# A two-block diffusion-style network on one core: squares in pairs, a gate moved behind its root, and later modulation steps

## The chip, the core and the metric

The kernel runs on one core of one Trainium2 chip. It is one program with five instruction streams: TensorE (PE, with its weight loads shown apart as PEld), VectorE (DVE), ScalarE (ACT), GpSimd (POOL) and SyncE (SP), which issues nearly all of the DMAs. The metric is the time of one execution on the device in microseconds; times shown are medians over runs, and one further execution was taken with the hardware profiler.

## The reference

The reference is two blocks of two layers each over 512 tokens of 1024 features, the first with 256 tokens of context beside them. Every layer is a norm with a modulation, a mixer, a gated residual, and in the first block a convolutional feed-forward network (FFN):

```python
mod_l = (silu_c @ ada_w[l] + ada_b[l])[:, None, :]
sh1, sc1, g1, sh2, sc2, g2 = jnp.split(mod_l, 6, axis=-1)
hl = modulate(xl, norm_mix_w[l], sh1, sc1)      # rms_norm(x, w) * (1 + scale) + shift
...
yl, yc = even_mixer(...) if l % 2 == 0 else odd_mixer(...)
xl = xl + g1 * yl
xl = xl + g2 * conv_ffn(modulate(xl, norm_ffn_w[l], sh2, sc2), ...)
...
def hgrn2_readout(o, g, onorm_w):
    o = rms_norm(o.transpose(0, 2, 1, 3), onorm_w).reshape(bsz, t_len, A_WIDTH)
    return (o * jax.nn.silu(g.astype(jnp.float32))).astype(g.dtype)
...
return rms_norm_2(x, final_g)                    # end of the second block
```

All of it is float32. The modulation is a product of one vector with a 1024 x 6144 matrix (1024 x 3072 in the second block); the matrix is read from memory once.

## The kernel before

Activations lie feature-major: 128 features on the partitions, tokens along the row, context first (256 + 512 = 768 tokens). A projection is exact to float32 by three passes: weight and activation are each split into a rounded high part and a rest, and TensorE adds wH·hH, wL·hH and wH·hL. So each weight block of 128 x 1024 is loaded by SP (`raw`), rounded by ACT (`wH`, L119) and subtracted by DVE (`wL`, L120); `W` is the stream of these blocks. `W.prep` issues the load and split of the next block, `W.take` hands a block out and calls `W.ahead(n)`, which prepares blocks until n are ready beyond the ones in use. The evacuation `evac` that is called behind the last pass of a block reads the sums from PSUM.

The stages, with their place in the span before: the norm of the inputs and first projections of mixer 0 (0 to 64 us); a weave of the gated linear attention, further projections and gates (64 to 396); its out-projection (405 to 477); the first FFN (477 to 1031); mixer 1 (1056 to 1305); the second FFN (1316 to 1665); and in the second block mixer 2 (to 2010) and mixer 3 with the final norm (to 2255).

`mixer0` begins with the squares of x0t in eight chunks, alternately on ACT (L655) and DVE (L653), and sums over the partitions by matmuls with a tile of ones, 256 and 512 tokens wide. `rsqrt` (L568) makes 1/sqrt as exp(-ln/2) on ACT (L574, L575) with one step of Newton on DVE: m (`rsm`, L573), z (`rsz`, L576), z times m (L577), r (L578). The gates come last in the weave: `evac_g` applies Silu to the projected gate (L754) and multiplies it onto o (L755). `gla.readout(h)` norms o of head h by such a root, in halves of 384 tokens. [...]

The modulation of layers to come is done beside the FFNs: a step takes a chunk of `raw` and multiplies it with the vector, one variant on DVE (L399) and one on ACT (L401) with its addition on GpSimd (L402). `ada_pace(every, start, end)` says at which modelled TensorE time (`self.pe`, in us, counted from the matmuls issued) steps are issued. `make` similarly splits certain weights early (L149 on ACT, L150 on DVE) and writes them back to memory (`make_next`, `make_every`):

```python
while self.pe >= self.make_next:
    with self.W.behind():
        next(self.make_gen, None)
    self.make_next += self.make_every
```

In the FFN, `gp` is the gate after its projection (L827), L831 to L834 are its convolution and Silu, L843 multiplies by the value (`hf`). In `finish`, the last residual's chunks (L995) are squared (L621) and added (L622), and behind the root each chunk is multiplied by its weight and the root (L1624) and sent out (L1626).

The order in which each engine does its instructions is made by a list scheduler when the program is built, from the order of the code, priorities and dependences; `issue_after(x)` keeps what stands in it behind the instruction x in that order. A changed line can therefore move its neighbours too.

## Time and profile before

| | |
|---|---|
| median of 3 runs | 2260.82 us (2260.49 to 2261.41) |
| profiled execution, its own time | 2257.02 us |
| span of the profiled execution | 2255.0 us |
| TensorE busy | 2183.5 us (97%) |
| DVE, ACT, GpSimd busy | 1548.8 us (69%), 1110.5 us (49%), 439.4 us (19%) |
| mean granted clock of TensorE | 0.991 |
| data moved | 293.92 MB, 130 GB/s on average |

The profiler records one execution; the difference of 2.0 us between its time and its span lies outside the first and last recorded instruction. In the chain of what ended last, each step is followed back to what released it. In the timeline the brackets at a row's end say how long its engine was idle before the row and which instruction released it. [...]

### The profile page before, as it was taken

To read this page: it belongs to the slowest core of one execution; us is meant where nothing else is said; L and a number is where in the kernel's file an instruction comes from. 1 tells how busy PE (TensorE), PEld (TensorE's weight loads), DVE (VectorE), ACT (ScalarE), POOL (GpSimd) and SP (SyncE) were. 2 spreads that over 40 slices of the span, in tenths; PEclk is the share of its full clock that TensorE was granted. 3 is DMA by queue.
4 is the path that set the end of the run, shared out by engine and by line. 5 is a ranking of instruction groups with operands and counts; after the bars stand their busy time and mean duration, and the time that the engine had idled before them with its cause. 6 is when DMAs were issued, how large, how long until landed. Compare 5 with 4: busy or idle time off the path is not lost.

```text
span 2255.0 us, 34813 instructions
## 1 busy us (share of the span) xinstructions
PE 2183.5 (97%) x13412; PEld 1879.8 (83%) x13412; DVE 1548.8 (69%) x2917; ACT 1110.5 (49%) x2110; POOL 439.4 (19%) x391
## 2 busy tenths in 40 slices
PE   8999999899999999999999999999999999989997
PEld 5988798798888888889889888887888887778876
DVE  5778767479766545557898685454556757868996
ACT  4444444355445434434676554343435545646772
POOL 0223222003334323330100023233210000001110
PEclk9999999999999999999999999999999999999999
DMA  9222311337776767631230135545435244122111
GB/s 329 85 94 85 103 48 48 103 108 269 247 237 214 252 217 241 207 110 50 83 99 1 38 127 163 159 143 167 152 123 198 96 142 139 38 75 80 57 48 38
DMA packets 105142, 293.92 MB, mean 130 GB/s; under 512 B 9232, under 2 KB 17424, under 8 KB 104976
## 3 DMA queue, kind: packets, MB, share of 16 engines
q1 hardware_dynamic: 104976, 291.70, 39.1%
q8 instruction: 105, 1.72, 0.3%
q14 instruction: 61, 0.50, 0.1%
HBM read 256.01 MB, written 35.65 MB: 129 GB/s over the span
## 4 chain that ended last, share of the span: by engine, by line
PE 85%; DVE 10%; ACT 3%; issue 2%; DMA 1%; POOL 1%; SPq 0%; DVEq 0%; ACTq 0%; POOLq 0%
PE b L437 81%; PE b L1306 2%; DVE wL L120 1%; DVE n_t L605 1%; DVE hL L607 1%; PE b L367 1%; PE b L1194 1%; PE b L415 0%; DVE st L1872 0%; ACT ptH L489 0%; POOL kt L1865 0%; DVE ptL L490 0%; DMA wL<-edL 0%; DVE ss L1062 0%; DVE fo L1624 0%
## 5 line engine op out<-in xcount | busy, mean ns | idle before, releaser
L437 PE MATMUL b<-hH,wH 128*128 128x256 f32 (+1 forms) x1912 | 596.6, 354 | 6.8 <-DVE hf L843 2.0
L437 PE MATMUL b<-hH,wL 128*128 128x256 f32 (+1 forms) x1912 | 592.1, 352 | 3.2 <-DVE wL L120 3.2
L437 PE MATMUL b<-hL,wH 128*128 128x256 f32 (+1 forms) x1912 | 588.2, 351 | 0.9 <-DVE hL L607 0.9
L437 PEld LDWEIGHTS b<-hH,wH 128*128 128x128 f32 x1912 | 357.1, 189 | 58.9 <-issue 7.0
L402 POOL TENSOR_TENSOR gacc<-gacc,raw 128x512 f32<-128x512 f32 x182 | 290.3, 1595 | 578.0 <-ACT raw L401 364.4
L437 PEld LDWEIGHTS b<-hH,wL 128*128 128x128 f32 x1912 | 360.8, 189 | 50.5 <-DVE wL L120 3.9
L437 PEld LDWEIGHTS b<-hL,wH 128*128 128x128 f32 x1912 | 360.1, 189 | 47.3 <-DVE hL L607 1.5
L119 ACT ACTIVATE wH<-raw 128x1024 fp32r<-128x1024 f32 (+4 forms) x238 | 244.7, 1029 | 254.2 <-PE b L437 242.7
L120 DVE TENSOR_TENSOR wL<-raw,wH 128x1024 fp32r<-128x1024 f32 (+4 forms) x238 | 298.7, 1256 | 37.4 <-ACT wH L119 35.7
L437 PE MATMUL b<-hidH,wL 128*128 128x512 f32 (+1 forms) x570 | 171.1, 344 | 0.0
L437 PE MATMUL b<-hidH,wH 128*128 128x512 f32 (+1 forms) x570 | 171.0, 344 | 0.0
L437 PE MATMUL b<-hidL,wH 128*128 128x512 f32 (+1 forms) x570 | 170.5, 343 | 0.0
L401 ACT ACTIVATE raw<-raw,csil 128x512 f32<-128x512 f32 x182 | 124.1, 714 | 57.7 <-DVE gacc L399 36.5
L437 PE MATMUL b<-yH,wH 128*128 128x256 f32 (+1 forms) x416 | 130.8, 331 | 12.6 <-ACT yH L489 12.6
L437 PE MATMUL b<-yH,wL 128*128 128x256 f32 (+1 forms) x416 | 130.5, 330 | 1.5 <-DVE wL L120 1.5
L437 PE MATMUL b<-yL,wH 128*128 128x256 f32 (+1 forms) x416 | 128.6, 328 | 0.0
L437 PEld LDWEIGHTS b<-hidH,wH 128*128 128x128 f32 x570 | 106.8, 188 | 14.9 <-issue 1.4
L437 PEld LDWEIGHTS b<-hidL,wH 128*128 128x128 f32 x570 | 107.1, 188 | 14.4 <-issue 0.2
L437 PEld LDWEIGHTS b<-hidH,wL 128*128 128x128 f32 x570 | 107.2, 188 | 13.8
L489 ACT ACTIVATE ptH<-b 128x384 fp32r<-128x384 f32 (+2 forms) x160 | 77.6, 499 | 69.4 <-PE b L1306 53.6
L490 DVE TENSOR_TENSOR ptL<-b,ptH 128x384 fp32r<-128x384 f32 (+2 forms) x160 | 89.2, 567 | 18.7 <-ACT ptH L489 17.7
L437 PE MATMUL b<-wH,hH 128*128 128x256 f32 x352 | 100.3, 286 | 1.6 <-ACT z L670 1.0
(370 smaller groups left out, 3979.0 us busy)
## 6 DMA issues: line engine op xcount, KB each, us to landing
raw<-in_weights_dram SPq DMA_DIRECT2D x199, 512.0 KB, 3.8
raw<-in_ada_w_dram SPq DMA_DIRECT2D x144, 512.0 KB, 4.3
er<-in_weights_dram SPq DMA_DIRECT2D x32, 512.0 KB, 4.5
edH<-eH SPq DMA_DIRECT2D x32, 512.0 KB, 4.9
edL<-er SPq DMA_DIRECT2D x32, 512.0 KB, 5.4
wL<-edL SPq DMA_DIRECT2D x32, 512.0 KB, 3.8
wH<-edH SPq DMA_DIRECT2D x32, 512.0 KB, 4.5
raw<-in_weights_dram SPq DMA_DIRECT2D x32, 448.0 KB, 3.5
```

The source lines that it names most:

```text
L119: self.last["H"] = nc.scalar.activation(h[:, :n], src, AF.Copy).ins
L120: self.last["L"] = nc.vector.tensor_tensor(l[:, :n], src, h[:, :n].bitcast(F32), op=ALU.subtract).ins
L367: nc.tensor.matmul(acc[32 * q:32 * q + 32, :], self.csil[:, k + a, :], raw[:, a, :, q, :], start=k + a == 0, stop=k + a == KD - 1)
L401: nc.scalar.activation(raw[:, a], raw[:, a], AF.Copy, scale=c)
L402: nc.gpsimd.tensor_tensor(acc[v], acc[v], raw[:, a], op=ALU.add)
L437: self.tail = self.nc.tensor.matmul(ps, lhsT, rhs, start=start, stop=stop, **kw).ins
L489: self.nc.scalar.activation(h, src, AF.Copy)
L490: self.nc.vector.tensor_tensor(l, src, h.bitcast(F32), op=ALU.subtract)
L605: nc.vector.scalar_tensor_tensor(t, x(j, s, e), A[:, j, v:v + 1], r, op0=ALU.mult, op1=ALU.mult)
L607: nc.vector.scalar_tensor_tensor(hL[j][:, s:e], t, b, h.bitcast(F32), op0=ALU.add, op1=ALU.subtract)
L1194: nc.tensor.transpose(ps[:, c], P[:, a, c], self.ident)
L1306: self.nc.tensor.transpose(ps[:, k * 128:(k + 1) * 128], P[:, k * 128:(k + 1) * 128], self.ident)
```

## The change

Six edits. (1) The squares of the first norm are added in pairs on DVE before the sums with ones, which makes eight such matmuls in place of sixteen; ACT now does six of the squares. (2) `rsqrt` issues Ln before m, takes a list of PSUM halves with one Exp over both, and keeps its Exp in `self.root`. (3) The last gate's Silu goes into tiles of its own (`z`) and is issued behind the Exp of the last readout, whose root is done in one piece. (4) `lin` calls `W.ahead(2)` behind the first evacuation of a first group that goes over all tokens at once (the out-projections). (5) The modulation steps of the FFNs start at 26 and 18 us instead of 8 and come every 6.9 us instead of 7.2; `make` starts at 26 instead of 2 and goes every 6.5 instead of 6.9. (6) In the final norm ACT multiplies the last 256 tokens by the weight as they come, and behind the root DVE does four multiplications of 512 columns instead of eight of 256.

```diff
@@ -464,6 +464,8 @@
                     with self.tc.high_priority(100):
                         for i in blocks:
                             evac(b0 + i, ps[i], part)
+                            if parts is segs and i == 0:
+                                self.W.ahead(2)
                 if end and after:
                     after(part[0])
 
@@ -570,9 +572,12 @@
         nc = self.nc
         w = r.shape[-1]
         m, z = scratch or (pool.tile([128, w], F32, name="rs" + i, tag="rs%s%d" % (i, w), bufs=1) for i in "mz")
-        nc.vector.tensor_scalar(m, x, -4.0 / n, -4 * EPS, op0=ALU.mult, op1=ALU.add)
-        nc.scalar.activation(r, x, AF.Ln, bias=self.eps[:, 0:1], scale=1.0 / n)
-        nc.scalar.activation(r, r, AF.Exp, bias=self.eps[:, 1:2], scale=-0.5)
+        xs = x if isinstance(x, list) else [x]
+        c = w // len(xs)
+        for i, v in enumerate(xs):
+            nc.scalar.activation(r[:, i * c:(i + 1) * c], v, AF.Ln, bias=self.eps[:, 0:1], scale=1.0 / n)
+            nc.vector.tensor_scalar(m[:, i * c:(i + 1) * c], v, -4.0 / n, -4 * EPS, op0=ALU.mult, op1=ALU.add)
+        self.root = nc.scalar.activation(r, r, AF.Exp, bias=self.eps[:, 1:2], scale=-0.5).ins
         nc.vector.tensor_tensor(z, r, r, op=ALU.mult)
         nc.vector.tensor_tensor(z, z, m, op=ALU.mult)
         nc.vector.scalar_tensor_tensor(r, z, 3.0, r, op0=ALU.add, op1=ALU.mult)
@@ -648,13 +653,16 @@
                 self.ada_load(nt, 12) if n == 4 else self.W.load()
         sums = [self.aux()[:, :e - s] for s, e, _, _ in SEG2]
         for j in range(KD):
-            sq = nt.tile([128, T], F32, name="n_sq", tag="n_sq", bufs=3)
-            if j % 2:
+            sq = nt.tile([128, T], F32, name="n_sq", tag="n_sq", bufs=4)
+            if j in (1, 5):
                 nc.vector.tensor_tensor(sq, xt[:, j], xt[:, j], op=ALU.mult)
             else:
                 nc.scalar.activation(sq, xt[:, j], AF.Square)
-            for (s, e, _, _), ps in zip(SEG2, sums):
-                self.mm(ps, self.ones, sq[:, s:e], j == 0, j == KD - 1)
+            if j % 2:
+                nc.vector.tensor_tensor(sq, prev, sq, op=ALU.add)
+                for (s, e, _, _), ps in zip(SEG2, sums):
+                    self.mm(ps, self.ones, sq[:, s:e], j == 1, j == KD - 1)
+            prev = sq
         r = nt.tile([128, T], F32, name="n_r")
         for (s, e, _, _), ps in zip(SEG2, sums):
             self.rsqrt(nt, r[:, s:e], ps, D)
@@ -750,7 +758,10 @@
 
         def evac_g(b, ps, part):
             for s, e, bank, _ in SEG2:
-                t = gt.tile([128, 512], F32, name="ut", tag="ut", bufs=1)
+                if b < 3:
+                    t = gt.tile([128, 512], F32, name="ut", tag="ut", bufs=1)
+                else:
+                    t = gt.tile([128, T], F32, name="z", tag="z", bufs=4)
                 nc.scalar.activation(t[:, :e - s], ps[:, bank, :e - s], AF.Silu)
                 nc.vector.tensor_tensor(o[:, b, s:e], o[:, b, s:e], t[:, :e - s], op=ALU.mult)
 
@@ -768,7 +779,14 @@
         self.psum(("mm", "aux"), mm=(0, 2, 1, 3), aux=(4, 6, 5))
         fill = itertools.chain(project(1), mixed(0), project(2), gated("u", 0, evac_u), project(3), mixed(1),
                                *[gated("u", i, evac_u) for i in range(1, 4)], *[gated("g", i, evac_g) for i in range(3)])
-        self.run(lin_v(0), self.weave(attend(), self.mixed_in(fill, self.ada_pe(24), 6.8), 178.0), gated("g", 3, evac_g))
+        self.run(lin_v(0), self.weave(attend(), self.mixed_in(fill, self.ada_pe(24), 6.8), 178.0))
+        root = self.root
+
+        def evac_g3(b, ps, part):
+            with self.tc.issue_after(root):
+                evac_g(b, ps, part)
+
+        self.run(gated("g", 3, evac_g3))
         self.close("h0")
         self.close("gt")
         self.dump("og", o)
@@ -860,10 +878,10 @@
             return ev
 
         total = 3 * NF * KD * 3 * T / 2400
-        self.ada_pace(7.2, 8.0, total - 16.0)
+        self.ada_pace(6.9, (26.0, 18.0)[l], total - 16.0)
         self.side, self.ada_fetch = self.open("side", n.side), True
         if l == 0:
-            self.make_gen, self.make_next, self.make_every = self.W.make(self.side, self.dram), self.pe + 2.0, 6.9
+            self.make_gen, self.make_next, self.make_every = self.W.make(self.side, self.dram), self.pe + 26.0, 6.5
         i0 = 0
         for gi, G in enumerate(FFN_GROUPS):
             st["H"], st["L"] = [], []
@@ -1613,16 +1631,26 @@
 
         nc = self.nc
         nt = self.open("nt", "right")
-        add, rstd = self.sumsq(nt, TL, self.xl)
+        sumsq, rstd = self.sumsq(nt, TL, self.xl)
+        fo = [nt.tile([128, 2, 256], F32, name="fo", tag="fo", bufs=8) for _ in range(8)]
+
+        def add(j, s, e):
+            sumsq(j, s, e)
+            if e == TL:
+                nc.scalar.activation(fo[4 + j // 2][:, j % 2], self.xl(j, TL - 256, TL), AF.Copy,
+                                     scale=self.vec("final_g", j, 1))
 
         def after(part):
             s, e, _, _ = part
             r = rstd(part)
             for j in range(0, KD, 2):
-                o = nt.tile([128, 2, 256], F32, name="fo", tag="fo", bufs=4)
-                for i in range(2):
-                    nc.vector.scalar_tensor_tensor(o[:, i], self.xl(j + i, s, e), self.vec("final_g", j + i, 1), r,
-                                                   op0=ALU.mult, op1=ALU.mult)
+                o = fo[j // 2 + (4 if s else 0)]
+                if s:
+                    nc.vector.tensor_tensor(o, o, r[:, None, :].to_broadcast([128, 2, 256]), op=ALU.mult)
+                else:
+                    for i in range(2):
+                        nc.vector.scalar_tensor_tensor(o[:, i], self.xl(j + i, s, e), self.vec("final_g", j + i, 1), r,
+                                                       op0=ALU.mult, op1=ALU.mult)
                 nc.sync.dma_start(self.out[:, j:j + 2, s:e], o)
 
         return SimpleNamespace(add=add, after=after)
@@ -1921,8 +1949,11 @@
 
             def ev():
                 r = big("qe")
-                for i, ps in enumerate(box["ps"]):
-                    self.rsqrt(pool, r[:, i * 384:(i + 1) * 384], ps, 128, [half_t("e", 2) for _ in range(2)])
+                if h < 3:
+                    for i, ps in enumerate(box["ps"]):
+                        self.rsqrt(pool, r[:, i * 384:(i + 1) * 384], ps, 128, [half_t("e", 2) for _ in range(2)])
+                else:
+                    self.rsqrt(pool, r, box["ps"], 128, [big(n, 2) for n in ("kc", "qc")])
                 nc.vector.scalar_tensor_tensor(o[:, h], o[:, h], self.vec("onorm"), r, op0=MUL, op1=MUL)
 
             return [(sq, pe, ev)]
```

Line numbers of the changed program are higher, by 2 to 31, than those of the one before. Below, rows stand in each engine's program order.

ACT at the end of the weave, before: the last readout's squares `ks`, then its roots in halves (`qe`), with the gate's Silu (`ut`) and a weight split.

```order
ACT_TABLE_LOAD
L574 ACTIVATE qe<-b_4106,eps 128x384
L575 ACTIVATE qe<-qe,eps 128x384
ACT_TABLE_LOAD
L754 ACTIVATE ut<-b_4134 128x256
ACT_TABLE_LOAD
L574 ACTIVATE qe<-b_4107,eps 128x384
L119 ACTIVATE wH<-raw 128x1024
L575 ACTIVATE qe<-qe,eps 128x384
ACT_TABLE_LOAD
L754 ACTIVATE ut<-b_4136 128x512
L489 ACTIVATE yH<-ym 128x768 x4
```

The same place in the changed program; `z` is the last gate's Silu, `ym` the first input of the out-projection.

```order
L1943 ACTIVATE ks<-o 128x768
ACT_TABLE_LOAD
L578 ACTIVATE qe<-b_4102,eps 128x384
L578 ACTIVATE qe<-b_4103,eps 128x384
L580 ACTIVATE qe<-qe,eps 128x768
ACT_TABLE_LOAD
L765 ACTIVATE z<-b_4124 128x256
L765 ACTIVATE z<-b_4126 128x512
L119 ACTIVATE wH<-raw 128x1024
L491 ACTIVATE yH<-ym 128x768 x4
```

Two loads of function tables less stand there, both halves of Ln and one Exp of 768 stand ahead of the Silus, and the weight split went behind them.

DVE early in the first FFN, before: the rest of the norm's hL, then `make`'s L150, modulation (L399), the convolution of two gates and the weight split that the next matmuls need.

```order
L607 SCALAR_TENSOR_TENSOR hL<-n_t,mods,hH 128x256 x2
L150 TENSOR_TENSOR er<-er,eH 128x1024
L399 SCALAR_TENSOR_TENSOR gacc<-raw,csil,gacc 128x512
L831 TENSOR_SCALAR a<-gp_4965,vecs 128x769
L399 SCALAR_TENSOR_TENSOR gacc<-raw,csil,gacc 128x512
L832 SCALAR_TENSOR_TENSOR a<-gp_4965,vecs,a 128x769
L831 TENSOR_SCALAR a<-gp_4966,vecs 128x769
L833 SCALAR_TENSOR_TENSOR a<-gp_4965,vecs,a 128x769
L832 SCALAR_TENSOR_TENSOR a<-gp_4966,vecs,a 128x769
L150 TENSOR_TENSOR er<-er,eH 128x1024
L833 SCALAR_TENSOR_TENSOR a<-gp_4966,vecs,a 128x769
L120 TENSOR_TENSOR wL<-raw,wH 128x1024
```

The same place in the changed program, where L849 to L851 are the convolution steps that were L831 to L833.

```order
L612 SCALAR_TENSOR_TENSOR hL<-n_t,mods,hH 128x256 x2
L849 TENSOR_SCALAR a<-gp_4955,vecs 128x769
L850 SCALAR_TENSOR_TENSOR a<-gp_4955,vecs,a 128x769
L849 TENSOR_SCALAR a<-gp_4956,vecs 128x769
L851 SCALAR_TENSOR_TENSOR a<-gp_4955,vecs,a 128x769
L850 SCALAR_TENSOR_TENSOR a<-gp_4956,vecs,a 128x769
L120 TENSOR_TENSOR wL<-raw,wH 128x1024
L851 SCALAR_TENSOR_TENSOR a<-gp_4956,vecs,a 128x769
L150 TENSOR_TENSOR er<-er,eH 128x1024
```

The two L150 and two L399 that stood ahead of the weight split are behind it.

TensorE at the end of the first sums, before (`n_sq` with ones are the sums, `raw` with csil the modulation, `hH` the first projection).

```order
L437 MATMUL b_130<-n_sq,ones 128x256
L437 MATMUL b_131<-n_sq,ones 128x512
L367 MATMUL b_181<-raw,csil 32x64 x32
L367 MATMUL b_222<-raw,csil 32x64 x32
L367 MATMUL b_270<-raw,csil 32x64 x32
L367 MATMUL b_307<-raw,csil 32x64 x32
L437 MATMUL b_365<-hH,wH 128x256
```

And in the changed program, from the third pair on.

```order
L437 MATMUL b_130<-n_sq,ones 128x256
L437 MATMUL b_131<-n_sq,ones 128x512
L367 MATMUL b_177<-raw,csil 32x64 x16
L437 MATMUL b_130<-n_sq,ones 128x256
L437 MATMUL b_131<-n_sq,ones 128x512
L367 MATMUL b_177<-raw,csil 32x64 x16
L367 MATMUL b_218<-raw,csil 32x64 x32
L367 MATMUL b_266<-raw,csil 32x64 x32
L437 MATMUL b_361<-hH,wH 128x256
L437 MATMUL b_363<-hH,wH 128x512
L367 MATMUL b_303<-raw,csil 32x64 x16
L437 MATMUL b_361<-hH,wL 128x256
```

Half of the first modulation group now stands ahead of the last pair's sums, and the fourth group is spread over the first projection's passes.

## Rows read from the trace of the kernel before

**Rows 1.** The page: busy time of TensorE, and the chain by engine.

```profile
PE 2183.5 (97%) x13412; PEld 1879.8 (83%) x13412; DVE 1548.8 (69%) x2917; ACT 1110.5 (49%) x2110; POOL 439.4 (19%) x391
...
PE 85%; DVE 10%; ACT 3%; issue 2%; DMA 1%; POOL 1%; SPq 0%; DVEq 0%; ACTq 0%; POOLq 0%
```

**Rows 2.** Windows: length; busy PE, PEld, DVE, ACT, POOL; clock, DMA share, GB/s.

```profile
6.50:20.00 13.50, 13.48 (x36) 7.55 (x38) 3.38 (x5) 2.85 (x4) 0.00 (x0) 1.00 1.05 383
20.00:30.30 10.30, 5.61 (x257) 4.65 (x256) 8.95 (x20) 6.40 (x11) 0.00 (x0) 0.80 1.07 370
30.30:45.90 15.60, 15.57 (x183) 12.60 (x183) 10.48 (x16) 6.69 (x9) 0.00 (x0) 0.92 1.04 386
```

**Rows 3.** Timeline of the start: start, duration, instruction, count, idle before and releaser.

```profile
6.51 13.52 PE L437 MATMUL b<-n_sq,ones 128*128 128x256 f32 x32 [6.51 <-ACT n_sq L655]
...
30.33 1.01 PE L437 MATMUL b<-hH,wH 128*128 128x256 f32 x2 [0.28 <-ACT hH L489]
```

**Rows 4.** The tile x0t: instructions (ns min/median/max, first and last start), landing.

```profile
L640 SPq DMA_DIRECT2D x0t<-in_xT_dram x4: 420/428/652, 1.2 to 2.6; - x4
L655 ACT ACTIVATE n_sq<-x0t x4: 842/842/843, 5.6 to 14.9; 128x768 f32<-128x768 f32 x4
L653 DVE TENSOR_TENSOR n_sq<-x0t x4: 957/958/959, 5.6 to 16.3; 128x768 f32<-128x768 f32 x4
...
DMA to landing us min/median/max: 4.4/6.6/8.7
```

**Rows 5.** Timeline of the last gate.

```profile
389.62 1.45 PE L437 MATMUL b<-ks,ones 128*128 128x384 f32 x4
...
397.16 0.58 ACT L574 ACTIVATE qe<-b,eps 128x384 f32<-128x384 f32 x1 [1.31 <-issue]
...
401.64 1.02 DVE L1926 SCALAR_TENSOR_TENSOR o<-o,vecs,qe 128x768 f32<-128x768 f32 x1
...
403.15 0.60 ACT L754 ACTIVATE ut<-b 128x512 f32<-128x512 f32 x1 [3.96 <-DVE o L755]
403.78 0.69 DVE L755 TENSOR_TENSOR o<-o,ut 128x512 f32<-128x512 f32 x1 [0.66 <-ACT ut L754]
...
405.46 1.01 PE L437 MATMUL b<-yH,wH 128*128 128x256 f32 x2 [9.79 <-ACT yH L489]
```

**Rows 6.** Windows, as Rows 2, behind the gate.

```profile
405.50:408.20 2.70, 2.70 (x9) 2.31 (x10) 2.70 (x4) 2.70 (x4) 0.00 (x0) 0.50 0.60 234
```

**Rows 7.** Timelines of DVE and TensorE in the first FFN.

```profile
501.09 1.22 DVE L150 TENSOR_TENSOR er<-er,eH 128x1024 fp32r<-128x1024 f32 x1 [4.97 <-ACT eH L149]
...
512.03 1.21 DVE L120 TENSOR_TENSOR wL<-raw,wH 128x1024 fp32r<-128x1024 f32 x1
...
513.30 0.50 PE L437 MATMUL b<-hH,wL 128*128 128x512 f32 x1 [2.11 <-DVE wL L120]
```

**Rows 8.** Windows, as Rows 2, of the first FFN.

```profile
477.00:520.00 43.00, 40.88 (x286) 38.03 (x285) 36.53 (x62) 23.70 (x42) 5.08 (x5) 0.96 0.57 196
520.00:620.00 100.00, 100.00 (x609) 86.74 (x608) 80.60 (x83) 50.37 (x69) 36.43 (x23) 1.00 0.74 256
```

**Rows 9.** Timelines of DVE and TensorE in the second FFN.

```profile
1337.23 1.52 DVE L831 TENSOR_SCALAR a<-gp,vecs 128x512 f32<-128x512 f32 x1
...
1342.05 0.51 PE L437 MATMUL b<-hH,wH 128*128 128x512 f32 x1 [1.96 <-DVE hf L843]
```

**Rows 10.** Timelines of TensorE and DVE in mixer 2's out-projection.

```profile
1994.42 0.68 DVE L622 TENSOR_TENSOR n_acc<-n_acc,n_sq 128x512 f32<-128x512 f32 x1
...
1994.56 0.50 PE L437 MATMUL b<-yH,wL 128*128 128x512 f32 x1 [1.50 <-DVE wL L120]
```

**Rows 11.** Timelines of TensorE, ACT and DVE in the tail.

```profile
2244.85 0.70 PE L437 MATMUL b<-n_acc,ones 128*128 128x256 f32 x2 [1.93 <-DVE n_acc L622]
...
2246.05 0.47 ACT L574 ACTIVATE n_r<-b,eps 128x256 f32<-128x256 f32 x1 [1.86 <-DVE rsm L573]
...
2248.48 3.26 DVE L1624 SCALAR_TENSOR_TENSOR fo<-xlat,vecs,n_r 128x256 f32<-128x256 f32 x8
```

## Prediction

> **What bounds the kernel now.** I read the page first: TensorE is busy 97% of the span, and 85% of the chain that ended last is its matmuls, nearly all at L437 [rows 1]. The change removes almost no TensorE work: 8 of 16 sums with ones in the start, four of which are 512 wide. So it can only gain where TensorE waits or runs at its lower clock. The second reading is therefore the list of TensorE's waits, and the third the clock by windows. Five places matter for this change, and in each the reader is to see who ended the wait: the start, where TensorE is full but with sums that nothing else can pass [rows 2, 3]; the last gate, one wait of 9.79 us [rows 5]; the first FFN, 2.11 us [rows 7]; the second FFN and the out-projection of the third mixer, 1.96 and 1.50 us [rows 9, 10]; and the tail after the last projection [rows 11].
>
> **Start: squares in pairs (gain 4.5 us, between 1.5 and 6).** From 6.5 to 20 us TensorE is busy 13.48 of 13.50 us, with 32 records of the sums in 13.52 us, 0.42 each [rows 2, 3]. After the change there are 16. They no longer set the pace: the last of the four transfers of x0t lands 2.6 + 8.7 = 11.3 us in; behind it stand two squares on ACT (0.84 each) and one addition on DVE, which I price as DVE's square of the same size, 0.96 [rows 4]. So the last pair is ready at 11.3 + 1.7 + 1.0 = 14.0, and its four records (1.7 us at 0.42, 3.4 at twice that, since the first sums go slower) end at 15.7 to 17.4, against 6.51 + 13.52 = 20.03. I take 16.9, some 3.1 earlier. The four additions cost DVE 3.8 us, and the two more squares on ACT 1.7: both lie under the landings. Behind the sums the first projection began at 30.33, 10.3 us after them [rows 3]. There DVE now takes the norm's products ahead of the weight split (1.21, [rows 7]) and ACT's Ln no longer stands behind rsm; that is worth another 1 to 2 us, so the projection begins some 5 earlier. Is its data there? The DMA engines are full until 45.9 (share 1.04 to 1.07, 370 to 386 GB/s, [rows 2]) and the order of the transfers is the same. Up to the end of that stretch the program takes x0t (3.1 MB), 16 pieces of modulation and three of weights (0.52 MB each) and 0.2 MB of vectors: 13.3 MB, at 0.38 MB/us about 35 us, and with the first 2.5 us 38, an estimate from those rows. TensorE was there at 45.9. The floor leaves 8 us, so it doesn't bind at the end; on the way, TensorE's new order puts half of a modulation group between two matmuls of the first projection, and waits there for its transfer. I take off half a microsecond for that: 4.5.
>
> TensorE's clock was granted at 0.80 in 20 to 30.3 and 0.92 in 30.3 to 45.9 [rows 2]. [...]
>
> **Last gate behind the root (gain 6.5 us, between 4.5 and 7.5).** Before: the sums of the last readout end at 391.07. The root goes in two halves; ACT puts a Silu between them, and Ln of the second half begins only at 397.16, with 1.31 us in which it waited for nothing shown, as behind a change of function. Then o at 401.64 (1.02 us), then the second Silu, which had waited 3.96 us for the multiplication that frees the one `ut` buffer, its multiplication at 403.78 (0.69), and TensorE goes on at 405.46 [rows 5]. After: Ln, Ln, one Exp of 768 and both Silus in a row. The first Ln begins when its sums end, about 390.5 (two of the four records); two at 0.58 and an Exp of 768, which I price at 0.85 between Silu's 0.60 for 512 and o's 1.02 for 768: root at 392.7. DVE's four steps of 768 at 1.02 end at 396.8, while ACT does the Silus into buffers of their own and one weight split. The two multiplications, 0.69 and about 0.4, end at 397.9. In before, TensorE began 1.0 us after the multiplication ended (405.46 - 404.47); that gives 398.9, or 6.55 earlier. The weight split that DVE now has between the gate and yL (1.21) puts yL at 400; TensorE has two passes of the first chunk before it needs yL, at half clock 1.6 us (398.9 to 400.5), so it hides; if it doesn't, it costs up to 1. I count the half clock behind the wait (405.5 to 408.2, granted 0.50, [rows 6]: 1.35 us) as still lost; if the shorter wait spares it, the gain goes to 7.5. The sum counts one thing more as zero: two changes of ACT's function fewer, since they are inside these times.
> By the row, a change costs 1.31 of idle. [...]
>
> **Later steps in the first FFN (gain 3.6, between 0 and 4.5).** DVE idles 4.97 us at 496 to 501, because the first `make` step L150 stands ahead of L831 and its input has only just come. All of DVE's queue is then late: wL runs 512.03 to 513.24, TensorE waits 2.11 us for it [rows 7], and the clock of that stretch is 0.96 of 43 us, 1.7 lost [rows 8]. With make from 26 us and modulation from 26, DVE's rows go from hL straight to L831: that spares the 4.97 of idle time and two L150 steps (1.22 each) and two of L399 ahead of wL. The gate's input, not DVE, then sets the end; wL would come some 3 us earlier, before the matmul that waited. I count 2.11 + 1.5. The same steps are now done in less time: every 6.9 and 6.5 instead of 7.2 and 6.9, with as many of them, so DVE's load rises by some 5% later on. DVE is busy 80.6% where it is fullest (520 to 620), and TensorE 100% [rows 8]: the room is 19%, so I price the denser pace at zero, and at rival 4 if the cover is gone.
>
> **Second FFN (gain 1.0, between -1 and 2).** L831 took 1.52 us at 1337.23, while GpSimd makes the additions of a modulation step, where another DVE step of that size takes 0.68 [rows 10]; hf is then late, and TensorE waits 1.96 [rows 9]. Modulation from 18 instead of 8 takes these additions away there. Against it, DVE's new order has two weight splits (1.21 each) between the steps of the norm just ahead. Net 1.0.
>
> **W.ahead(2) (gain 1.5, between 0 and 1.8).** At 1994.56 TensorE waits 1.50 for a wL that stands behind four residual additions and is late [rows 10]. Now the splits for the next two blocks are issued after the first evacuation; the other projections of this form had no such wait. The residuals behind it come 1.2 us later, and only the norm's squares wait for them.
>
> **Tail (gain 1.4, between 1.0 and 1.8).** Ln began at 2246.05, though the sums ended at 2245.55: Ln ahead of rsm gives 0.46. Behind the root eight multiplications take 3.26 [rows 11]; four of 512 columns at 0.68 with some overlap, as DVE's addition of that size [rows 10], take 2.5: 0.8. Two fewer ahead of the last n_acc: 0.2. ACT's eight extra multiplications lie in its waits (1.86 in that row).
>
> Ln first in the other norms, and the scheduler's new orders in the weave and the mixers, I count as zero: none of these places is edited, and a single late instruction there is worth what one was elsewhere, 1.5 to 2.1 us [rows 7, 9, 10]; two of them either way make the bounds, 4 less or 4 more.
>
> **Sum:** 4.5 + 6.5 + 3.6 + 1.0 + 1.5 + 1.4 = 18.5. The profiled execution took 2257.0 us (span 2255.0 and 2.0 around it), so 2238.5; the median of the runs shown is 3.8 above that execution, which gives 2242.3: I predict 2242.
>
> **The rivals.** (1) The start's gain is given back: with half the sums TensorE idles between pairs, stays at half clock through the 5 us of projection behind them, and waits for the pieces of modulation. For it: the clock of 0.80 after idling [rows 2]. Against: the first projection was at half clock already. Gain 1.5 instead of 4.5: 2245.3; 13%. (2) At the gate TensorE then waits for yL behind the weight split, or Ln still behind a change of function: 4 instead of 6.5, 2244.8; 10%. (3) The change doesn't do what it says outside the gate: other orders of DVE bring new waits in the weave and the mixers, as many as the FFN terms save; that leaves the start, the gate and the tail less 4, 2252; 12%. (4) The other side: DVE's cover in the first FFN fails. There each late wL costs what the one at 513 did, 2.11 + 1.7 = 3.8. Five of them undo the gain of 18.5; from the seventh the kernel is slower by over 0.2% (4.5 us, about what a measurement of this kernel can tell from no change). At eight: 2273. For it: the pace is denser over all of 500 us. Against: no such wait from 520 to 620 at 80.6%. Undone 4%, slower 4%. (5) More than the sum: the half clock is spared at the gate, and the reorders help: 2238; 7%.
>
> **Numbers.** The forecast has 50%, by itself 2239 to 2246. The range takes in rivals 1, 2, 3 and 5 and leaves out rival 4 and the edges: 2236 to 2252. Faster 0.92, same 0.04, slower 0.04.
>
> **What the profile after would show.** Start: 16 records of sums, ended before 17.5, and the stretch that ended at 45.9 ending near 41. Gate: Ln, Ln, Exp without a Silu between, TensorE again by 399.3 less what the start gained. FFN: no wait at the first wL, clock near 1.00 there. Out-projection: no 1.5 us wait. Tail: four multiplications, some 10.6 us from TensorE's last projection matmul to the end instead of 12.1. The prediction is wrong if TensorE's waits of the same size stand elsewhere, above all before wL in the first FFN, or if the start ends above 43.

## The result, and the profile after

The changed kernel takes 2235.26 us (median of 4 runs, 2230.33 to 2236.51) against 2261.11 us: a ratio of 0.9881 with an interval of 0.9864 to 0.9898, 23 to 31 us less. The forecast was 2242 us, with a range of 2236 to 2252. The direction was right, the time lies just below the range, and two of the sum's terms were far off in opposite directions.

The page of the changed kernel: span, busy time of the engines, chain by engine.

```profile
span 2233.8 us, 34775 instructions
...
PE 2177.2 (97%) x13396; PEld 1875.4 (84%) x13396; DVE 1551.3 (69%) x2912; ACT 1117.5 (50%) x2119; POOL 443.5 (20%) x391
...
PE 80%; DVE 9%; issue 7%; ACT 2%; DMA 1%; POOL 0%; DVEq 0%; SPq 0%; ACTq 0%; POOLq 0%
```

TensorE's busy time fell by 6.3 us against [rows 1], the span by 21.2. So about 15 us came out of waits. Stage by stage, the start gave nothing. Windows of its first 46 us, columns as in [rows 2]:

```profile
7.80:17.00 9.20, 9.13 (x61) 4.57 (x65) 3.83 (x4) 4.67 (x7) 0.00 (x0) 1.00 1.06 378
17.00:20.00 3.00, 1.56 (x96) 1.23 (x87) 2.44 (x8) 2.49 (x4) 0.00 (x0) 1.00 1.02 388
20.00:30.30 10.30, 5.99 (x134) 4.41 (x134) 9.72 (x17) 6.37 (x9) 0.00 (x0) 0.67 1.07 370
30.30:45.90 15.60, 15.60 (x196) 11.71 (x187) 7.29 (x12) 4.09 (x6) 0.00 (x0) 1.00 1.05 391
```

TensorE's timeline there, where [rows 3] had one block of sums and the projection at 30.33:

```profile
7.82 6.86 PE L437 MATMUL b<-n_sq,ones 128*128 128x256 f32 x12 [7.82 <-DVE n_sq L662]
...
15.32 1.56 PE L437 MATMUL b<-n_sq,ones 128*128 128x256 f32 x4
...
22.04 0.65 PE L367 MATMUL b<-raw,csil 128*32 128x64 f32 x32 [3.11 <-DVE gacc L373]
24.29 1.08 PE L367 MATMUL b<-raw,csil 128*32 128x64 f32 x32 [1.60 <-DMA raw<-in_ada_w_dram]
25.45 1.01 PE L437 MATMUL b<-hH,wH 128*128 128x256 f32 x2
...
45.64 0.64 PE L367 MATMUL b<-raw,csil 128*32 128x128 f32 x16
```

The sums are 16 records, done by 16.9, and the projection begins at 25.45, 4.9 us earlier. But TensorE now waits 3.11 and 1.60 us for pieces of the modulation, which come no earlier (the fifth and sixth land at 21.9 and 24.2 us, before at 21.4 and 22.9), the clock of 20 to 30.3 is 0.67 instead of 0.80, and the modulation that the second half of the norm needs ends at 46.3, where it ended at 45.9 before.

The last gate, ACT, DVE and TensorE, against [rows 5]:

```profile
388.47 1.45 PE L437 MATMUL b<-ks,ones 128*128 128x384 f32 x4
389.31 1.23 ACT L578 ACTIVATE qe<-b,eps 128x384 f32<-128x384 f32 x2 [1.99 <-PE b L437]
...
390.57 0.94 ACT L580 ACTIVATE qe<-qe,eps 128x768 f32<-128x768 f32 x1
...
394.31 0.87 ACT L765 ACTIVATE z<-b 128x256 f32<-128x256 f32 x2 [2.80 <-PE b L437]
394.52 1.02 DVE L1957 SCALAR_TENSOR_TENSOR o<-o,vecs,qe 128x768 f32<-128x768 f32 x1
...
397.66 0.61 PE L437 MATMUL b<-yH,wH 128*128 128x256 f32 x2 [3.15 <-ACT yH L491]
```

Ln over both halves, one Exp, the Silus behind it, and a wait of 3.15 us instead of 9.79. From the first matmul of the sums with ones to the first of the out-projection it is 9.19 us instead of 15.84: 6.65 less, where the forecast had 6.55.

In the first FFN TensorE is idle for 0.1 us in all, so nothing is left of the wait of [rows 7]; in the second none of [rows 9] is. In the out-projection of mixer 2, the third of the four mixers, the wait for wL of [rows 10] is gone. TensorE's waits from 1960 to 1990 us (line, releaser, us in total, times, longest):

```profile
PE b L437 <- ACT yH L491: 2.8, 1, 2.8
PE b L437 <- ACT ptH L491: 0.2, 1, 0.2
```

The tail, TensorE, ACT and DVE against [rows 11], and then the DMA view of 2227 to 2233.8, GB/s in 40 slices, and the four last issues with their size and time to landing:

```profile
2224.04 0.70 PE L437 MATMUL b<-n_acc,ones 128*128 128x256 f32 x2 [1.77 <-DVE n_acc L627]
...
2224.78 0.47 ACT L578 ACTIVATE n_r<-b,eps 128x256 f32<-128x256 f32 x1 [0.85 <-PE b L437]
...
2227.20 2.50 DVE L1649 TENSOR_TENSOR fo<-fo,n_r 128x512 f32<-128x512 f32 x4
...
GB/s 0 0 0 0 0 0 0 0 0 0 36 307 331 301 379 350 319 307 392 344 307 331 373 343 338 337 361 343 313 54 0 0 0 0 0 0 0 0 0 0
...
out_dram<-fo SPq DMA_DIRECT2D x4, 256.0 KB, 2.5
```

Ln starts 0.04 us after the sums and four multiplications take 2.50, as priced. The last four transfers of 256 KB then run without a break at some 340 GB/s, 0.77 us each, while DVE delivers one every 0.63 (one every 0.82 before, by [rows 11]). From the first multiplication to the end it is 6.6 us now and 6.5 to 6.6 before, so the quicker multiplications gain nothing at the end, where the queue is now the slower of the two.

### The profile page after: what moved, and what is told of

It reads as the page before. It is cut to its first block, busy times and chain, and to the rows that moved or that the text cites. A ratio compares the mean times of both kernels' runs of the same rounds, so it can differ in the third digit from the quotient of the medians.

```text
span 2233.8 us, 34775 instructions
## 1 busy us (share of the span) xinstructions
PE 2177.2 (97%) x13396; PEld 1875.4 (84%) x13396; DVE 1551.3 (69%) x2912; ACT 1117.5 (50%) x2119; POOL 443.5 (20%) x391
## 4 chain that ended last, share of the span: by engine, by line
PE 80%; DVE 9%; issue 7%; ACT 2%; DMA 1%; POOL 0%; DVEq 0%; SPq 0%; ACTq 0%; POOLq 0%
PE b L437 77%; PE b L1324 1%; DVE wL L120 1%; PE b L367 1%; DVE hL L612 1%; DVE n_t L610 1%; PE b L1212 1%; PE b L415 0%; DVE st L1900 0%; DVE z L1739 0%; ACT ptH L491 0%; DVE ss L1080 0%; DVE ptL L492 0%; DVE e L1886 0%; PE b L1787 0%
## 5 line engine op out<-in xcount | busy, mean ns | idle before, releaser
L849 DVE TENSOR_SCALAR a<-gp,vecs 128x769 f32<-128x769 f32 (+1 forms) x44 | 30.0, 681 | 139.7 <-ACT gp L845 139.7
```

The source lines that it names most:

```text
L849: nc.vector.tensor_scalar(a, gp[:, 1:1 + L], cw(1, i), cb(i), op0=ALU.mult, op1=ALU.add)
```

## The experiments

Each stage runs from its first matmul to that of the next; in the kernel before, the bounds are 0, 65.2, 389.6, 405.5, 475.5, 1103.8, 1313.5, 1695.4, 1950.9 and 2016.9 us, so the first FFN's row takes in the first projections of mixer 1. All are single profiled executions. Two of the same kernel differ by up to 1.5 us in a stage (the first two columns) and by 2.0 in the start (the two runs without pairs below, 63.7 and 65.7), so only larger differences are read. The columns with Ln first have 12 of TensorE's records, some 2 us of work at the stage's mean of 0.2 each, behind the bound at 1695 instead of ahead of it (1825 or 1826 in the second FFN's stage, elsewhere 1837 or 1838); the second FFN and mixer 2 are therefore read together.

| us | before | before again | pairs | gate only | Ln only | Ln and gate | steps only | all, m first | all |
|---|---|---|---|---|---|---|---|---|---|
| start | 65.2 | 64.5 | 65.8 | 64.4 | 65.7 | 64.4 | 64.5 | 66.6 | 65.3 |
| weave | 324.4 | 323.4 | 324.1 | 326.0 | 323.3 | 323.8 | 324.1 | 325.2 | 323.1 |
| last gate | 15.8 | 15.8 | 15.8 | 9.8 | 11.5 | 9.2 | 15.8 | 9.8 | 9.2 |
| out-projection 0 | 70.0 | 70.6 | 70.3 | 70.3 | 70.7 | 71.1 | 70.0 | 70.6 | 71.1 |
| first FFN | 628.3 | 629.6 | 628.9 | 629.2 | 627.2 | 627.2 | 624.7 | 624.0 | 623.0 |
| mixer 1 | 209.7 | 210.6 | 209.6 | 209.6 | 209.4 | 208.9 | 209.8 | 209.9 | 210.3 |
| second FFN | 381.8 | 381.8 | 383.4 | 384.6 | 376.0 | 376.6 | 378.4 | 378.8 | 376.7 |
| mixer 2 | 255.6 | 254.7 | 255.5 | 254.6 | 256.0 | 255.9 | 254.8 | 254.7 | 255.3 |
| these two together | 637.4 | 636.6 | 638.9 | 639.1 | 632.0 | 632.4 | 633.2 | 633.4 | 632.0 |
| mixer 2's out-projection | 66.0 | 64.5 | 64.8 | 64.8 | 63.1 | 63.5 | 64.8 | 63.5 | 61.3 |
| mixer 3 and tail | 238.2 | 238.0 | 239.3 | 239.5 | 238.3 | 236.6 | 239.1 | 238.3 | 238.5 |
| **timed, ratio to before** | 1 | 1.0001 | 1.0000 | 0.9977 | 0.9925 | 0.9922 | 0.9971 | 0.9923 | 0.9881 |

**The kernel before, again.** No edit.

> The kernel before, unchanged, once more. Theory A (its first profiled execution, 2257.0 us, was a quick draw): ratio 1.000, and this profile is 2259 to 2261 us, longer than the first by stretches at half clock and by waits whose length changes, not by other instructions. Rival B (the profiler takes some 4 us off this kernel, but none off the changed one): again 2256 to 2258 us, at the same places.

The timed ratio is 1.0001 (0.9991 to 1.0012), the profile 2255.68 us, the lowest of ten runs between that and 2264.64. Theory A's 2259 was missed, and B is not shown either: other profiles (2259.39 with the pairs alone, 2235.58 of the changed kernel) lie a little above their medians, and another execution of this kernel, not the profiled one, took 2255.74. What follows is narrower: one profiled execution of this kernel can lie 4 us below its median. Whether the 3.8 us that the prediction carried over from before to after was a draw stays open, since both profiles of this kernel lie 4 to 5 us low; in the changed kernel it is not there.

**The start.** Pairs alone; then the changed kernel without pairs, twice, the second time beside the changed kernel on one chip; then the changed kernel with one pair's sums only.

```diff
 # pairs alone (in part; the whole is in the diff of the change)
...
+            if j % 2:
+                nc.vector.tensor_tensor(sq, prev, sq, op=ALU.add)
...
 # one pair only: the sums of the other three are left out, the divisor is D // 4
-                for (s, e, _, _), ps in zip(SEG2, sums):
-                    self.mm(ps, self.ones, sq[:, s:e], j == 1, j == KD - 1)
+                for (s, e, _, _), ps in zip(SEG2, sums) if j == KD - 1 else ():
+                    self.mm(ps, self.ones, sq[:, s:e], True, True)
...
```

> The kernel before with the pairs of squares alone. Theory A (the start's end is set by the pieces of modulation, which come when they came, and by TensorE's order behind them, so that sums done earlier only make TensorE idle earlier): the first projection begins near 25.5 us instead of 30.3, the weave near 65.3 as in both kernels, and the time is within 1 us of before. Rival B (the pairs gain what the prediction gave them, and another edit took it back): the weave begins 4 to 5 us earlier and the time is 4.5 us less.

> The changed kernel with the squares as before, one sum with ones for each chunk. Theory A (the pairs gain nothing anywhere): the weave begins within 1 us of 65.3, and the time is within 2 us of the changed kernel's, 2234 to 2237. Rival B (the pairs are worth their 4.5 us in the changed kernel, where other edits spend it): 2239 to 2241.

> The changed kernel once more, beside the same without pairs on one chip. Theory A (the pairs are neutral): both within 1 us of each other. Rival B (the pairs cost: TensorE idles 4 us more in the start and the clock falls there and in the weave): this one 1.5 to 3 us slower than the one without pairs. Its ratio to before 0.987 to 0.990.

> The changed kernel with the squares as before, a second time, now beside the changed kernel. Theory A: within 1 us of it. Rival B: 1.5 to 3 us less, and the better version of the two; the weave begins near 64 us.

> The changed kernel, where only the last pair goes through the sums with ones; the other three pairs are left out of the norm's sum, and its divisor is a quarter. Theory A (TensorE's work ahead of 30 us is not what ends the start): the weave still begins at 65 to 65.5 us, though 12 of 16 records of the sums are gone. Rival B (these sums are on the path): it begins 1 to 5 us earlier.

Pairs alone: ratio 1.0000 (0.9991 to 1.0010). Without pairs 0.9880 (0.9866 to 0.9895), and the second time 0.9883 (0.9868 to 0.9898) beside 0.9887 (0.9871 to 0.9904) for the changed kernel: 2232.80 and 2233.36 us. With one pair's sums alone a single run took 2234.24 us. The pairs neither gain nor cost. With pairs alone the projection begins at 26.56 (expected near 25.5) and the weave at 65.8, and without them the weave of the changed kernel begins at 63.7, earlier than expected, and at 65.7. With one pair's sums alone the sums still end at 17.2, since they cannot begin before the last squares, and the projection begins at 25.44 as in the changed kernel: that run takes work from TensorE, but brings nothing earlier. Windows of the start with pairs alone:

```profile
0.00:20.00 20.00, 10.57 (x144) 5.97 (x144) 9.06 (x18) 8.15 (x13) 0.20 (x4) 1.00 0.95 341
20.00:30.30 10.30, 5.47 (x113) 3.96 (x117) 9.70 (x17) 6.33 (x9) 0.00 (x0) 0.67 1.07 370
30.30:45.90 15.60, 15.60 (x200) 11.76 (x192) 7.30 (x12) 4.09 (x6) 0.00 (x0) 1.00 1.05 392
45.90:65.80 19.90, 17.83 (x164) 14.68 (x163) 10.30 (x17) 12.54 (x19) 3.27 (x4) 1.00 0.50 166
```

And with one pair's sums alone:

```profile
0.00:20.00 20.00, 5.83 (x124) 3.77 (x128) 8.56 (x17) 8.34 (x13) 0.20 (x4) 1.00 0.94 340
20.00:30.30 10.30, 7.33 (x149) 5.49 (x141) 8.90 (x18) 6.20 (x8) 0.00 (x0) 0.57 1.08 372
30.30:45.90 15.60, 15.60 (x191) 11.73 (x183) 8.16 (x13) 4.09 (x6) 0.00 (x0) 0.96 1.05 390
45.90:65.70 19.80, 17.42 (x163) 14.32 (x161) 10.22 (x17) 12.46 (x19) 4.06 (x4) 1.00 0.48 164
```

The first window shows what is taken from TensorE: 13.48 us busy before, 10.57, then 5.83. From 30.3 to 45.9 it is busy throughout in both, as in [rows 2], and the weave begins at 65.8 and 65.7 against 65.2. TensorE's idle time up to there is 12.2, 16.3 and 19.6 us: with the pairs what the sums no longer take is idled. The clock of 20 to 30.3 is 0.80, 0.67 and 0.57, but from 20 to 45.9 the pairs lose no more by it (length times one less the clock: 3.3 us before, 3.4 with pairs, 5.1 with one pair): the stretch at half clock (granted 0.50, from 26.1 to 32.9 us before, from 23.3 to 30.1 in the changed kernel) only comes earlier. In these three profiles the clock of 20 to 30.3 is the lower the less TensorE did up to 20 us (13.48, 10.57 and 5.83); why is not shown.

**The roots and the gate.** Ln ahead of m alone; that with the gate edit; the gate edit with m first; and all six edits with m first.

```diff
 # Ln only (rsqrt); "m first" has the two lines of the loop the other way round
-        nc.vector.tensor_scalar(m, x, -4.0 / n, -4 * EPS, op0=ALU.mult, op1=ALU.add)
-        nc.scalar.activation(r, x, AF.Ln, bias=self.eps[:, 0:1], scale=1.0 / n)
...
+        for i, v in enumerate(xs):
+            nc.scalar.activation(r[:, i * c:(i + 1) * c], v, AF.Ln, bias=self.eps[:, 0:1], scale=1.0 / n)
+            nc.vector.tensor_scalar(m[:, i * c:(i + 1) * c], v, -4.0 / n, -4 * EPS, op0=ALU.mult, op1=ALU.add)
...
 # gate
+                    self.rsqrt(pool, r, box["ps"], 128, [big(n, 2) for n in ("kc", "qc")])
...
+            with self.tc.issue_after(root):
+                evac_g(b, ps, part)
```

> The kernel before with Ln ahead of m in every root and the last gate behind one root of 768. Theory A (the gate's term was right): the 9.79 us wait becomes some 3.2, the out-projection's first matmul comes 6.6 us earlier plus up to 1 us from the weave, and the tail 0.5 less: 7 to 8 us less. Rival B (the orders of the weave and the later stages, which move with it, gain as much again): over 10 us less.

> The kernel before with nothing but Ln ahead of m in every root. Theory A (what the run with Ln and gate gained behind the gate comes from Ln: in the second FFN's norm DVE then does its three root steps between the weight splits instead of behind them): the waits of 0.93, 0.66 and 1.96 us in the second FFN shrink to under 1 us together, that FFN takes some 377 us instead of 382, the gate still waits 9.8, and the whole is 6 to 9 us less. Rival B (the gate moved the schedule of all that follows by chance): the second FFN stays at 382 and the whole is within 2 us of before.

> The changed kernel with m ahead of Ln again in every root, the other edits kept. Theory A (Ln ahead of m is the largest part, and shares the second FFN's waits with the later steps): the gate waits 4 to 5 us instead of 3.15, the FFNs lose 1 to 3 us, the third mixer's out-projection 1 to 2, the tail 0.5: slower than the changed kernel by 5 to 10 us, 2240 to 2246. Rival B (the order in the roots matters only where the later steps and the gate are not changed): within 2 us of the changed kernel.

> The kernel before with the last gate behind one root of 768, m still ahead of Ln. Theory A (the gate edit by itself gives what was predicted for it less the 0.5 us that Ln ahead saves): the wait of 9.79 becomes 3.5 to 4.5, the FFNs and the third mixer are as before, 5 to 7 us less. Rival B (most of the gate's gain came from Ln as well): 2 to 3 us less, with a wait over 6 us.

The pair of edits gave 0.9922 (0.9908 to 0.9937), over twice what theory A had, so Ln was run alone: 0.9925 (0.9910 to 0.9940), some 17 us, where 6 to 9 were expected. The gain comes with Ln's two lines and needs no gate edit. The gate alone gave 0.9977 (0.9966 to 0.9987), 5 us, with a wait of 3.74; and all edits but Ln 0.9923 (0.9909 to 0.9938), 2243.04 us, 8 to 10 slower than the changed kernel on that chip (its gate waits 3.74, where 4 to 5 were expected). But the two lines also change the order that the list scheduler makes around them. With Ln alone the gate had been expected to keep its wait of 9.8 us; it waits 5.42:

```profile
391.01 1.11 ACT L578 ACTIVATE qe<-qe,eps 128x384 f32<-128x384 f32 x2
...
394.89 0.38 ACT L757 ACTIVATE ut<-b 128x256 f32<-128x256 f32 x1 [2.76 <-PE b L437]
...
400.51 1.01 PE L437 MATMUL b<-yH,wH 128*128 128x256 f32 x2 [5.42 <-ACT yH L489]
```

Both Ln and both Exp now stand ahead of the first Silu, which the gate edit was to bring about. So 4.4 us at the gate come with Ln alone by a new order; where the gate edit fixes the order, Ln or m first makes 0.6 there (9.2 and 9.8). No run swaps the two reads and keeps all else in place. What the swap itself does is seen in the second FFN's norm. Before: the sums, then DVE, then ACT.

```profile
1315.83 0.70 PE L437 MATMUL b<-n_acc,ones 128*128 128x256 f32 x2
...
1317.67 1.27 DVE L607 SCALAR_TENSOR_TENSOR hL<-n_t,mods,hH 128x256 fp32r<-128x256 f32 x3
1318.86 0.42 DVE L573 TENSOR_SCALAR rsm<-b 128x256 f32<-128x256 f32 x1
1319.19 2.35 DVE L120 TENSOR_TENSOR wL<-raw,wH 128x1024 fp32r<-128x1024 f32 x2
1321.46 0.42 DVE L576 TENSOR_TENSOR rsz<-n_r 128x256 f32<-128x256 f32 x1
...
1319.31 0.47 ACT L574 ACTIVATE n_r<-b,eps 128x256 f32<-128x256 f32 x1 [1.01 <-DVE rsm L573]
```

With Ln alone:

```profile
1310.08 0.70 PE L437 MATMUL b<-n_acc,ones 128*128 128x256 f32 x2
...
1310.87 0.46 ACT L576 ACTIVATE n_r<-b,eps 128x256 f32<-128x256 f32 x1
...
1312.31 0.42 DVE L577 TENSOR_SCALAR rsm<-b 128x256 f32<-128x256 f32 x1
...
1313.04 0.41 DVE L579 TENSOR_TENSOR rsz<-n_r 128x256 f32<-128x256 f32 x1
1313.38 1.22 DVE L120 TENSOR_TENSOR wL<-raw,wH 128x1024 fp32r<-128x1024 f32 x1
1314.51 0.41 DVE L580 TENSOR_TENSOR rsz<-rsz,rsm 128x256 f32<-128x256 f32 x1
```

Before, rsm stands in DVE's row behind the norm of other chunks and starts 2.3 us after the sums; Ln waits for it (1.01), Exp for Ln, and the first step on the root stands behind two weight splits. With Ln first, ACT starts 0.09 us after the sums, and rsm follows where DVE has room. Of the stage's 5.9 us less, TensorE's waits are 3.1, and the 12 records that run behind its bound some 2. The tile view of rsm in the kernel before says how much waited for it in all (us, times):

```profile
  ACT n_r L574: 22.0, 12
```

With Ln alone nothing waits for rsm any more, and DVE waits for Ln, 6.5 us in 4 times; with all edits but Ln it is 20.0 us in 12 again. The 22 us are ScalarE's idle time and no price: the gain was 17 alone and 8 to 10 beside the other edits. The order with m first holds in the gate edit, where Ln stands behind both rsm, here in `kc`:

```profile
391.26 1.20 DVE L576 TENSOR_SCALAR kc<-b 128x384 f32<-128x384 f32 x2 [2.90 <-PE b L437]
...
391.85 1.23 ACT L577 ACTIVATE qe<-b,eps 128x384 f32<-128x384 f32 x2 [2.61 <-DVE kc L576]
...
400.19 0.76 PE L437 MATMUL b<-yH,wH 128*128 128x256 f32 x2 [3.74 <-ACT yH L489]
```

Here m and Ln read the same sums and neither reads what the other writes, but the one that stands second is seen to wait for the other (Ln for m 22.0 us in 12 times with m first, m for Ln 6.5 us in 4 with Ln first), so the one that the longer chain needs belongs first. Why it waits is not shown.

**Later steps.** Edit 5 alone.

```diff
-        self.ada_pace(7.2, 8.0, total - 16.0)
+        self.ada_pace(6.9, (26.0, 18.0)[l], total - 16.0)
...
-            self.make_gen, self.make_next, self.make_every = self.W.make(self.side, self.dram), self.pe + 2.0, 6.9
+            self.make_gen, self.make_next, self.make_every = self.W.make(self.side, self.dram), self.pe + 26.0, 6.5
```

> The kernel before with the later modulation and make steps alone. Theory A (both FFNs gain by it, and more than predicted): the first FFN 5 to 6 us, the second 4 to 5 (the waits of 1.96, 0.93 and 0.66 us go together), 10 to 11 us less. Rival B (this edit gives the predicted 4.6, and the rest of what the FFNs gained came from Ln standing ahead in their norms): 4 to 5 us less, with the waits of 0.93 and 0.66 in the second FFN's norm still there.

0.9971 (0.9958 to 0.9985): 3 to 9 us, between the theories. The first FFN takes 4 to 5 us less (its wait of 2.11 for wL is gone), the second 3 to 4. In its norm stood, before, two waits besides the one of [rows 9]:

```profile
1324.68 0.39 PE L437 MATMUL b<-hH,wH 128*128 128x256 f32 x1 [0.93 <-ACT hH L606]
...
1329.02 0.39 PE L437 MATMUL b<-hL,wH 128*128 128x256 f32 x1 [0.66 <-DVE hL L607]
```

With the later steps alone 1.96 and 0.66 are gone, and of 0.93 half is left:

```profile
1319.35 0.39 PE L437 MATMUL b<-hH,wH 128*128 128x256 f32 x1 [0.48 <-ACT hH L606]
```

The L831 of 1.52 us in [rows 9] is one of 22 of that size in the second FFN; it alone runs beside a GpSimd addition, and the others take 0.50 to 0.55. With the later steps such a long one (1.54) stands at 1341.6, where TensorE does not wait for it.

**Earlier splits.** `W.ahead(2)` alone, as in the diff of the change.

> The kernel before with the earlier splits of two blocks alone. Theory A: the wait of 1.2 to 1.5 us for wL in the third mixer's out-projection goes, and a loss at half clock with it: 1.5 to 3 us less. Rival B (the residuals and squares that come later cost as much): within 1 us.

0.9993 (0.9983 to 1.0002), a median 2.1 us lower: unclear. In its profile the wait for wL is gone, and the out-projection takes 62.4 us, 2 to 4 less than in the five runs with m first and without this edit (63.5 in the one with m first and all other edits). The tail's edit was not run alone; but from its sums on the tail takes 9.7 us with Ln alone and 9.8 with all edits, 10.2 before.

## Why the prediction was wrong

The step that failed on one side is the start. That "the projection begins some 5 earlier" was right; that the stage then ends 4.5 earlier was not. I counted the bytes up to the end of the stretch, found room and stopped there. The count held (the sixteenth piece of the modulation lands at 39.6 us, by the estimate 38); what I left out is TensorE's own work behind the earlier start. Up to the end of that piece it now has 192 records of the modulation and 63 of the projection, before 128 and 55, and runs 4.7 us of them at half clock, before 2.6; from 30.3 us it is full in both, and the piece is done at 46.3 instead of 45.9. In the fourteen profiles of this case the projection begins between 25.4 and 30.3 us, and that piece is done between 44.5 and 47.4, not sooner where the projection begins sooner. Work removed ahead of that only makes TensorE idle, and a window with TensorE 100% busy did not show that this work was on the path. Which part the new order, the clock and the late pieces each have is not shown by a run. It was rival 1's mechanism in its waits for the pieces, to the whole 4.5 instead of 3; over the start the half clock took no more than before, it only falls on more of this work.

The step that failed on the other side is "Ln first in the other norms ... I count as zero". It is the largest single edit: 17 us alone and 8 to 10 in the presence of the others, which take some of the same waits away. Rival 5 had the direction ("the reorders help"), at 7% and 4 us. I had its price in view: in the tail's row Ln waits for rsm, and I used that wait there and nowhere else. By stage, with all m-first runs of the same edits beside it, Ln alone gives 1 to 2 in the weave, 4.4 at the gate, 1 to 2 in the first FFN, 5 to 7 in the second FFN and mixer 2 together (1.4 beside the later steps) and 1.5 to 2 in the third mixer's out-projection; of these, one by one, only the gate and the second FFN are clear of what two profiles of one kernel differ by.

The other terms: the gate had its mechanism and its size (6.65 for 6.5), though 0.6 of it is Ln's. Alone, Ln brings 4.4 of the same wait, by the scheduler's order. The first FFN's 3.6 was 4 to 5 by the later steps and 5 to 7 with Ln. The second's 1.0 was 3 to 4 by the steps alone, and 5 with Ln (with mixer 2): I took the norm's order, weight splits between the root's steps, for a loss, and the rows above show it as the gain, since the root was no longer late. W.ahead's 1.5 stands at 2 by its stage, unclear by time. The tail's 1.4 came to 0.6, from TensorE's last projection matmul to the end 11.5 us instead of 12.1, where 10.6 was forecast: Ln gave its 0.46; the multiplications were quicker by what was priced, and the last transfers took it back. Rival 4, a DVE too full for the denser pace, did not happen: no wait over 0.1 us in the first FFN.

The last error is the 3.8 us carried from before to after. The two profiled executions differ by 2257.02 - 2235.58 = 21.4 us where the sum had 18.5, so the terms, wrong as they were singly, miss by only 2.9 together, which is luck. The other 4.1 of the 7.0 us come from the offset: the changed kernel's profiled execution lies 0.3 above its median, not 3.8 below.

## What to carry to other kernels

Where two engines read the same sums, look which of the two reads the longer chain hangs on and put it first, in every place that uses the helper: a wait that a tile view sums over the whole span (22 us in 12 times here) is worth a run of its own, though it is not its price. A full engine is not yet the path: before pricing removed work, ask what the stage after it waits for. And edits that cure the same wait do not add: at the last gate the gate edit takes 6.1 us off, Ln first 4.4, both 6.6. Over the whole, pairs, gate, Ln, steps and splits gave 0, 5, 17, 7 and 2 us alone, 31 in all, and 26 together with the tail's edit; the intervals are too wide to show that difference.

## What the runs showed of the hardware

Which stretches fall to half clock behind a short wait changes between executions of one program: the third mixer's out-projection lost 5.3 us of full clock (length times one less the granted clock) in the first profile of before, 1.9 in the second, and TensorE's busy time there was 59.4 and 58.3 us. So an engine's busy time in one profile is not a constant of the kernel, and a difference of 2 to 4 us between two profiles needs timed runs.

A VectorE step beside a GpSimd addition took up to nearly three times as long: of L831 at 128x512 in the second FFN, 1.52 us where an addition ran through 0.9 of it, 0.50 to 0.55 for the other 21. In the changed kernel two ran so, 1.53 and 0.69 us.

In the profile before, ScalarE has fifteen idle stretches of over 0.3 us without a releaser up to the last gate, and each is 1.31 us long; at the last of them, in [rows 5], the order of the program has an ACT_TABLE_LOAD.
